# Up projections of two squared-relu MLPs: block products of seven quarter products instead of eight

## The chip, the cores and the metric

The kernel runs on one core of a Trainium2 chip, in one launch. Times are microseconds on the device. The core's engines run side by side and are ordered by semaphores: TensorE (PE: matmuls; PEld is its loading of the stationary operand), VectorE (DVE), ScalarE (ACT), GpSimd (POOL), and SyncE (SP), whose queue issues the large weight loads. Matmuls accumulate in PSUM banks; everything else lies in SBUF tiles of 128 partitions.

## What is computed

A first block (latent attention, banded attention and a hierarchical mixture of experts) feeds a second one of two layers. The second block ends each layer with a squared-relu MLP, and these two MLPs are all that the change is about:

```python
def sq_relu_mlp(h, w_up, w_down):
    return jnp.square(jax.nn.relu(h @ w_up)) @ w_down

def second_block(...):
    for l in range(DEPTH_2):                        # 2 layers
        h = rmsnorm(x, g_attn[l])
        x = x + dsa_mixer(h, ...) if l == 0 else x + nsa_mixer(h, ...)
        x = x + sq_relu_mlp(rmsnorm(x, g_mlp[l]), w_up[l], w_down[l])
        if l == 0:
            kv_shared = shared_kv(x, ...)
    return rmsnorm(x, g_final)
```

x has 512 tokens and 1024 features in float32; w_up is 1024x4096, w_down 4096x1024.

## The kernel before

**Layout.** The activations lie transposed: `xT[:, k]` is chunk k (128 of the 1024 features) by 512 tokens. A projection makes 128 output features by 512 tokens at a time, a feature block, by adding eight chunk products in one PSUM bank.

**Split float32.** Every float32 product is three matmuls of a faster float32 form (`mm3`): high by high, high by low, low by high part. `split` makes the two parts of a tile: a cast on ScalarE (L60), then a subtract of the tile and the cast on VectorE (L66). This is done for each weight tile of 128x1024 after its DMA (`wraw`, four buffers; `wload`), for the normalized input, and for each hidden block.

**One MLP.** `mlp(l)` takes the 32 hidden blocks in four groups q. A group is eight up blocks, which give hidden blocks `hidh`/`hidl`, then eight down steps that consume them and add to the residual. An up block is 24 matmuls of 512 columns (`proj_gen`); its evacuation `ev_up` is relu on ScalarE, square on VectorE, and a split. `proj_gen` splits the weight of block n+1 while it issues block n. In the second MLP the down projection has the hidden blocks as stationary operand, and the residual is first transposed to token-major tiles `xn`.

**Around it.** The normalization has no pass of its own. `norm_block` scales the residual by the gain and splits it (`xh`, `xl`) as each block of the attention's output projection (`a_w_o`, `b_w_o`) arrives; the row statistics are applied after the down projection (`rb2`, `rn2`, squares of the reciprocal deviation, since squared relu is homogeneous). `hook1` computes these statistics during the first group, after up block 1; `hook2`, after up block 3, makes the broadcast (first MLP) or the 32 transposes and eight ScalarE copies (second).

**Order.** A tile scheduler keeps, on each engine, an order of its own for the instructions that this code issues, and adds the semaphores. Each engine runs its list in that order. X, O and P are pools of tiles of 128x512; a pool's next tile waits for the last reader of the one that it replaces.

Of the kernel before, what the change touches and what calls it, by code (L numbers as in the profile page):

```python
# [34 lines left out]
class Kern:  # L35
# [20 lines left out]
    def split(self, src, hi, lo, scale=None, pool=False):  # L56

        nc = self.nc
        if scale is None:
            nc.scalar.copy(hi, src)  # L60
        else:
            nc.scalar.activation(out=hi, in_=src, func=AF.Copy, scale=scale)
        if pool:
            return nc.gpsimd.tensor_tensor(out=lo, in0=src, in1=fv(hi), op=OP.subtract)  # L64
        if scale is None:
            return nc.vector.tensor_tensor(out=lo, in0=src, in1=fv(hi), op=OP.subtract)  # L66
        return nc.vector.scalar_tensor_tensor(out=lo, in0=src, scalar=scale, in1=fv(hi), op0=OP.mult, op1=OP.subtract)
# [116 lines left out]
            acc = self.square(acc, b, rows)  # L184
        return acc

    def norm(self, gain=None, both=None):

        st = Ctx()
        st.gain, st.both, st.acc, st.acc2, st.xh, st.xl = gain, both, None, None, [], []  # L190
        self.nx = st
        return st

    def norm_block(self, k):
        st, x = self.nx, self.xT[:, k]
        if st.gain is not None:
            st.xh.append(self.X("xh", F32R))
            st.xl.append(self.X("xl", F32R))
            self.split(x, st.xh[k], st.xl[k], st.gain[:, k:k + 1])
        st.acc = self.square(st.acc, x)  # L200
        if st.both is not None:
            st.acc2 = self.square(st.acc2, x, scale=st.both[:, k:k + 1], pool=True)

    def norm_nat(self, exp=False):
        st = self.nx
# [1013 lines left out]
    def dsa(self):  # L1219
        nc, A, xT, small = self.nc, self.A, self.xT, self.small  # L1220
        st = self.nx
# [23 lines left out]
        r1, r2, rr, rr2 = s4("r1"), s4("r2"), s4("rr"), s4("rr2")  # L1245
# [205 lines left out]
    def mlp(self, l):  # L1451
        nc, xT = self.nc, self.xT
        st = self.nx
        xh, xl = st.xh, st.xl
        if l == 0:
            self.norm(self.vec("g_kv_shared"))
        else:
            xn = [[None] * 2 for _ in range(4)]

        def hook1():  # L1460
            st.nat = self.nat_rstd(self.sums([st.acc]), D)
            if l == 1:
                st.rn2 = self.small.tile([128, 4], F32, tag="rn2", name="rn2")
                self.mul(st.rn2, st.nat, st.nat)

        def hook2():
            if l == 0:
                rb = self.bcast_rows(st.nat)
                st.rb2 = self.P("rb2", 1)
                self.mul(st.rb2, rb, rb)  # L1470
                return
            for t in range(4):
                for half in range(2):
                    pt = self.bank("t")
                    for k in range(4):
                        nc.tensor.transpose(pt[:, 128 * k:128 * k + 128], xT[:, 4 * half + k, 128 * t:128 * t + 128], self.ident)  # L1476
                    a = self.O("xn")
                    nc.scalar.copy(a, pt)
                    xn[t][half] = a
        if l == 1:  # L1480
            gf = self.ph.tile([128, D], F32, name="gf")
            g = self.A["g_final_2"]
            nc.sync.dma_start(gf, bass.AP(tensor=g.tensor, offset=g.offset, ap=[[0, 128], [1, D]]))
            ss = self.small.tile([128, 8], F32, tag="ssf", name="ssf")

        def finish(t0, t1):
            n = t1 - t0
            s4 = self.small.tile([128, n], F32, tag="s4", name="s4")
            v = ss[:, 2 * t0:2 * t1].rearrange("p (t h) -> p t h", h=2)
            nc.vector.tensor_tensor(out=s4, in0=v[:, :, 0], in1=v[:, :, 1], op=OP.add)  # L1490
            y = self.small.tile([128, n], F32, tag="y4", name="y4")
            self.col_rstd(s4, y, D)
            for t in range(t0, t1):

                a, b = xn[t]
                nc.scalar.activation(out=a, in_=a, func=AF.Copy, scale=y[:, t - t0:t - t0 + 1])
                nc.sync.dma_start(self.out[128 * t:128 * t + 128, 0:512], a)
                nc.vector.scalar_tensor_tensor(out=b, in0=b, scalar=y[:, t - t0:t - t0 + 1], in1=gf[:, 512:1024], op0=OP.mult, op1=OP.mult)
                nc.sync.dma_start(self.out[128 * t:128 * t + 128, 512:1024], b)

        for q in range(4):
            hh, hl = [], []

            def ev_up(b, ps):
                r = self.P("r", 2)
                nc.scalar.activation(out=r, in_=ps, func=AF.Relu)
                self.mul(r, r, r)
                a, c = self.X("hidh", F32R), self.X("hidl", F32R)
                self.split(r, a, c)
                hh.append(a)  # L1510
                hl.append(c)
            up = self.proj_gen(f"w_up{l}", range(8 * q, 8 * q + 8), xh, xl, ev_up)
            for n, _ in enumerate(up):
                if q == 0 and n == 1:
                    hook1()
                if q == 0 and n == 3:
                    hook2()
            if l == 0:
                def ev_down(b, ps):
                    b = b % 8  # L1520
                    t = self.P("dt", 2)
                    self.mul(t, ps, st.rb2)
                    nc.vector.tensor_tensor(out=xT[:, b], in0=xT[:, b], in1=t, op=OP.add)
                    if q == 3:
                        self.norm_block(b)
                self.proj_tr("w_down0", range(8 * q, 8 * q + 8), hh, hl, ev_down)
            else:
                for half in range(2):
                    last = q == 3 and half == 1
                    ps = [self.bank(g) for g in "sstt"]  # L1530
# [102 lines left out]
    def nsa(self, rb, kc, vc, kh, kl, vs):  # L1633
        nc, A, xT, ph = self.nc, self.A, self.xT, self.ph
# [158 lines left out]
def prep(inp):  # L1793
    g = {k: np.asarray(v) for k, v in inp.items()}
    m = {}
# [11 lines left out]
    o = np.arange(4000)  # L1807
# [24 lines left out]
    for l in range(2):  # L1832
        m[f"g_attn{l}"] = cols(g["g_attn_2"][l])
        m[f"g_mlp{l}"] = cols(g["g_mlp_2"][l])
        m[f"w_up{l}"] = chunks(g["w_up_2"][l])

    m["w_down0"] = g["w_down_2"][0].reshape(4, 8, 128, 8, 128).transpose(0, 3, 2, 1, 4).reshape(32, 128, 8, 128)

# [41 lines left out]
```

## Time and profile before

| | us |
|---|---|
| median of 3 runs | 2015.24 (2012.69 to 2016.48) |
| the profiled execution | 2013.01 |
| its span | 2011.2 |
| TensorE busy in it | 1915.0 (95%) |
| VectorE, ScalarE, GpSimd busy | 948.4, 733.1, 258.5 |
| mean granted TensorE clock | 0.977 of full speed |

The span runs from the first to the last recorded instruction; 1.8 us of the execution's time lie around it. The first MLP's up phases start at 1015.13, 1104.01, 1191.05 and 1278.09 us, with a down phase after each; those of the second at 1648.32, 1740.46, 1827.50 and 1914.54. Matmul records are longer than the distance between two matmuls, since matmuls overlap in TensorE: the pitch from start to start is what one costs.

### The profile page before, as it was taken

To read this page: it belongs to the slowest core of one execution; us is meant where nothing else is said; L and a number is where in the kernel's file an instruction comes from. 1 tells how busy PE (TensorE), PEld (TensorE's weight loads), DVE (VectorE), ACT (ScalarE), POOL (GpSimd) and SP (SyncE) were. 2 spreads that over 40 slices of the span, in tenths; PEclk is the share of its full clock that TensorE was granted. 3 is DMA by queue.
4 is the path that set the end of the run, shared out by engine and by line. 5 is a ranking of instruction groups with operands and counts; after the bars stand their busy time and mean duration, and the time that the engine had idled before them with its cause. 6 is when DMAs were issued, how large, how long until landed. Compare 5 with 4: busy or idle time off the path is not lost.

```text
span 2011.2 us, 26048 instructions
## 1 busy us (share of the span) xinstructions
PE 1915.0 (95%) x9802; PEld 1461.1 (73%) x9802; DVE 948.4 (47%) x2004; ACT 733.1 (36%) x1333; POOL 258.5 (13%) x330
## 2 busy tenths in 40 slices
PE   8999999979998867899999999999999999999998
PEld 6777778865544324558888888887789988888886
DVE  5677764461000025378454444465266554444343
ACT  3555552222111124357442323242355534233233
POOL 2212210020000024245100000000134300000001
PEclk9999999989999989799999999999999999999999
DMA  7523633138999994001233233224510032333221
GB/s 257 189 97 124 217 132 117 62 136 347 356 369 384 369 383 163 32 16 39 84 94 95 95 102 98 95 95 146 177 46 32 22 105 84 94 97 103 95 94 64
DMA packets 88224, 286.76 MB, mean 143 GB/s; under 512 B 12128, under 2 KB 13152, under 8 KB 88096
## 3 DMA queue, kind: packets, MB, share of 16 engines
q1 hardware_dynamic: 82624, 273.01, 39.1%
q10 hardware_dynamic: 4320, 7.87, 1.0%
q0 software_dynamic: 1152, 4.19, 0.6%
q8 instruction: 79, 1.29, 0.3%
q14 instruction: 49, 0.40, 0.1%
HBM read 274.02 MB, written 11.01 MB: 142 GB/s over the span
## 4 chain that ended last, share of the span: by engine, by line
PE 57%; DVE 2%; POOL 1%; issue 0%; ACT 0%; DVEq 0%; POOLq 0%; ACTq 0%
PE mm L49 37%; PE s L49 8%; PE o L49 5%; PE t L49 5%; PE t L244 1%; DVE sc L1336 0%; DVE p L230 0%; DVE m L1335 0%; POOL dw L1318 0%; PE t L1476 0%; DVE dg L162 0%; POOL cql L64 0%; POOL wl L64 0%; DVE wl L66 0%; DVE selb L1340 0%
## 5 line engine op out<-in xcount | busy, mean ns | idle before, releaser
L60 ACT CAST wh<-wr 128x1024 fp32r<-128x1024 f32 (+1 forms) x222 | 230.9, 1041 | 579.3 <-PE mm L49 303.7
L66 DVE TENSOR_TENSOR wl<-wr,wh 128x1024 fp32r<-128x1024 f32 (+1 forms) x216 | 264.0, 1222 | 312.7 <-ACT wh L60 311.8
L49 PE MATMUL mm<-xh,wh 128*128 128x512 f32 (+1 forms) x640 | 252.7, 395 | 0.0
L49 PE MATMUL mm<-xh,wl 128*128 128x512 f32 (+1 forms) x640 | 250.4, 391 | 0.0
L49 PE MATMUL mm<-xl,wh 128*128 128x512 f32 (+1 forms) x640 | 250.0, 391 | 0.0
L49 PE MATMUL s<-wm,xg 128*64 128x512 f32 x544 | 142.2, 609 | 11.6 <-DMA wm<-in_w_gu 11.6
L49 PEld LDWEIGHTS mm<-xh,wh 128*128 128x128 f32 (+1 forms) x640 | 120.0, 188 | 28.2 <-issue 2.2
L49 PEld LDWEIGHTS mm<-xh,wl 128*128 128x128 f32 (+1 forms) x640 | 120.0, 188 | 26.0
L49 PEld LDWEIGHTS mm<-xl,wh 128*128 128x128 f32 (+1 forms) x640 | 120.0, 187 | 25.3 <-issue 0.5
L233 ACT ACTIVATE p<-p,mx 128x128 f32<-128x128 f32 (+3 forms) x160 | 89.7, 561 | 93.5 <-DVE mx L232 89.4
L49 PEld LDWEIGHTS s<-wm,xg 128*64 128x64 f32 x544 | 43.3, 140 | 90.8 <-issue 66.4
L970 DVE TENSOR_TENSOR hid<-hid,s 128x256 f32<-128x256 f32 x17 | 7.2, 421 | 205.9 <-ACT hid L969 205.9
L49 PE MATMUL mm<-hidh,wh 128*128 128x512 f32 x256 | 99.6, 389 | 0.0
L49 PE MATMUL mm<-hidl,wh 128*128 128x512 f32 x256 | 99.6, 389 | 0.0
L49 PE MATMUL mm<-hidh,wl 128*128 128x512 f32 x256 | 99.6, 389 | 0.0
L235 POOL TENSOR_SCALAR p<-p,mx 128x128 f32<-128x128 f32 (+3 forms) x96 | 59.4, 622 | 156.5 <-DVE mx L234 111.7
L49 PE MATMUL mm<-hh,wh 128*128 128x512 f32 x192 | 77.9, 407 | 1.1 <-ACT hh L60 1.1
L49 PE MATMUL mm<-hl,wh 128*128 128x512 f32 x192 | 76.0, 396 | 0.8 <-DVE hl L66 0.8
L49 PE MATMUL mm<-hh,wl 128*128 128x512 f32 x192 | 75.4, 393 | 0.0
L49 PE MATMUL mm<-d,h2h 128*128 128x256 f32 (+1 forms) x288 | 70.5, 289 | 3.8 <-ACT xg L1011 2.8
L230 DVE CUSTOM_DVE_ANT_0 p<-s,ms 128x256 f32<-128x256 f32 (+3 forms) x128 | 61.2, 487 | 24.1 <-PE s L49 22.1
L244 PE MATMUL t<-ident,p 128*128 128x128 f32 x400 | 68.5, 278 | 3.8 <-POOL p L235 3.7
(575 smaller groups left out, 3995.8 us busy)
## 6 DMA issues: line engine op xcount, KB each, us to landing
wm<-in_w_gu SPq DMA_DIRECT2D x136, 512.0 KB, 7.1
wm<-in_w_dn SPq DMA_DIRECT2D x68, 512.0 KB, 7.4
wr<-in_w_up SPq DMA_DIRECT2D x64, 512.0 KB, 3.5
wr<-in_w_down SPq DMA_DIRECT2D x64, 512.0 KB, 3.5
wr<-in_w_ada SPq DMA_DIRECT2D x48, 512.0 KB, 4.1
wr<-in_w_in SPq DMA_DIRECT2D x22, 512.0 KB, 3.6
wr<-in_cmp_w SPq DMA_DIRECT2D x16, 512.0 KB, 3.8
ydr<-y ACTq DMA_DIRECT2D x30, 256.0 KB, 6.3
```

The source lines that it names most:

```text
L49: self.nc.tensor.matmul(ps, lhsT=l, rhs=r, start=start, stop=stop)
L60: nc.scalar.copy(hi, src)
L66: return nc.vector.tensor_tensor(out=lo, in0=src, in1=fv(hi), op=OP.subtract)
L230: nc.vector.tensor_tensor_reduce(out=p[:, :n], in0=s[:, :n], in1=master[:, c0:c0 + n], scale=1.0, scalar=-3.0e38, op0=OP.add, op1=OP.max, ...
L233: nc.scalar.activation(out=p[:, :n], in_=p[:, :n], func=AF.Exp, bias=mx[:, 1:2], accum_out=mx[:, 2:3])
L235: nc.gpsimd.tensor_scalar(p[:, :n], p[:, :n], mx[:, 3:4], 1.0 if gate is None else gate, op0=OP.mult, op1=OP.mult)
L244: nc.tensor.transpose(ps[:, b], p[:, b], self.ident)
L970: nc.vector.tensor_tensor(out=hid, in0=hid, in1=ps[:, 256:512], op=OP.mult)
```

## The change

The up projection takes the feature blocks in pairs. Features (K) are divided into even and odd chunks, the pair into its two blocks, the tokens into two halves of 256: a 2x2 block product, which is made of seven quarter products instead of eight, each of 4 chunks and 256 columns. For this, sums of weight quarters (`weights7`, on GpSimd) and differences of input quarters (`factors`, on GpSimd, made where `norm_block` made `xh` and `xl`) are split as before, and the seven products are combined into the two blocks by ScalarE copies, VectorE adds with an operand in PSUM and GpSimd adds (`products7`). The order of the products is 1, 2, 6, 5, 3, 7, 4. The weights are laid out with the even chunks first (`echunks`).

```diff
     def norm_block(self, k):
         st, x = self.nx, self.xT[:, k]
-        if st.gain is not None:
+        if st.x7 is not None:
+            self.factors(st.x7, k, x, st.gain[:, k:k + 1])
+        elif st.gain is not None:
...
+    def factors(self, x7, k, x, scale):
...
+        f = self.O("f")
+        nc.scalar.activation(out=f, in_=x, func=AF.Copy, scale=scale)
+
+        def pair(space, n1, n2, j1, j2, src):
+            hi, lo = space("xh", F32R), space("xl", F32R)
+            self.split(src, hi, lo)
+            x7.f[n1][j1], x7.f[n2][j2] = (hi[:, a], lo[:, a]), (hi[:, b], lo[:, b])
+        sub = lambda out, p, q: nc.gpsimd.tensor_tensor(out=out, in0=p, in1=q, op=OP.subtract)
+        if k % 2 == 0:
...
+            self.split(f[:, a], *[t[:, c] for t in x7.t0])
+            x7.f[1][j] = x7.t0[0][:, c], x7.t0[1][:, c]
+            x7.even, x7.t12 = f, self.O("t12")
+            sub(x7.t12[:, a], f[:, b], f[:, a])
+            return
+        pair(self.X, 2, 3, j, j, f)
+        t12, t43 = x7.t12, self.O("t43")
+        sub(t12[:, b], f[:, b], t12[:, a])
+        pair(self.X, 5, 6, j, j, t12)
+        sub(t43[:, b], f[:, b], x7.even[:, b])
+        sub(t43[:, a], f[:, a], t12[:, b])
+        pair(self.X, 4, 7, j, j, t43)
+
+    def weights7(self, name, b0, b1):
+        nc = self.nc
+        r0, r1 = self.wraw(name, b0), self.wraw(name, b1)
+        tt = lambda out, p, q, op: nc.gpsimd.tensor_tensor(out=out, in0=p, in1=q, op=op)
+        e, o = slice(0, 4), slice(4, 8)
+        s12, s34 = [self.ph.tile([128, 8, 128], F32, tag="ws", name="ws", bufs=2) for _ in range(2)]
+        tt(s12[:, e], r1[:, e], r1[:, o], OP.add)
+        tt(s12[:, o], s12[:, e], r0[:, e], OP.subtract)
...
+        split(self.wp, "w", 2, r0, 1, 2)
+        yield
+        tt(s34[:, e], r0[:, e], r1[:, e], OP.subtract)
+        tt(s34[:, o], r0[:, o], s12[:, o], OP.subtract)
+        split(self.ph, "s", 3, s12, 5, 6)
+        yield
+        split(self.ph, "s", 3, r1[:, o], 4, None)
+        split(self.ph, "s", 3, s34, 7, 3)
+        yield w
...
+            def product(n):
...
+                ps = self.bank(("mm", "s", "t")[banks % 3], (128, 256))
+                banks += 1
+                for j in range(4):
+                    self.mm3(ps, w[n][0][:, j], w[n][1][:, j], *x7.f[n][j], j == 0, j == 3)
+                return ps
...
+            c1, c2 = self.C("c"), self.C("c")
+            p1 = part(product(1))
+            add(c1[:, a], product(2), p1)
+            next(ahead, None)
+            u2 = part(product(6))
+            add(u2, u2, p1, True)
+            p5 = part(product(5))
+            u4 = add(part(), u2, p5, True)
+            add(c1[:, b], product(3), u4)
+            evac(bs[0], c1)
+            next(ahead, None)
+            u3 = add(part(), product(7), u2)
+            add(c2[:, b], u3, p5, True)
+            add(c2[:, a], product(4), u3)
+            evac(bs[1], c2)
+            yield
...
         if l == 1:
...
+            hook2()
...
-            def ev_up(b, ps):
-                r = self.P("r", 2)
-                nc.scalar.activation(out=r, in_=ps, func=AF.Relu)
-                self.mul(r, r, r)
-                a, c = self.X("hidh", F32R), self.X("hidl", F32R)
-                self.split(r, a, c)
...
+            def ev_up(b, c):
+                if b % 2:
+                    nc.vector.scalar_tensor_tensor(out=c, in0=c, scalar=0.0, in1=c, op0=OP.max, op1=OP.mult)
+                else:
+                    nc.scalar.activation(out=c, in_=c, func=AF.Relu)
+                    nc.scalar.activation(out=c, in_=c, func=AF.Square)
...
+            up = self.products7(f"w_up{l}", [(b, b + 1) for b in range(8 * q, 8 * q + 8, 2)], st.x7, ev_up)
             for n, _ in enumerate(up):
-                if q == 0 and n == 1:
+                if q == 0 and n == 0:
                     hook1()
-                if q == 0 and n == 3:
+                if q == 0 and n == 1 and l == 0:
                     hook2()
```

`part(src)` is a ScalarE copy of a product to SBUF, and `add(..., True)` an add on GpSimd. Left out of the diff are the places where buffers now lie, and the final gain, whose load is issued after the last group's up blocks instead of at the MLP's start.

What this makes of VectorE's list at the end of a down phase and the start of the next up phase of MLP 1 (`dt` and `xT` are the down step's residual update, `wl` the low part of a weight tile). Before:

```order
L1175 TENSOR_TENSOR dt<-mm,rb_8906 128x512
L1523 TENSOR_TENSOR xT<-xT,dt 128x512
L66 TENSOR_TENSOR wl<-wr,wh 128x1024 x2
L1175 TENSOR_TENSOR r<-r 128x512
L66 TENSOR_TENSOR hidl<-r,hidh 128x512
L66 TENSOR_TENSOR wl<-wr,wh 128x1024
```

After, the stretch of one pair in the first group of that MLP (`sl` is the low part of a weight sum or of the odd half of the second block's weight, `u` and `c` are 256-column parts; `mm`, `s` and `t` are the banks that the products take in turn):

```order
L300 TENSOR_TENSOR c<-s,u 128x256
L300 TENSOR_TENSOR u<-t,u 128x256
L66 TENSOR_TENSOR sl<-wr,sh 128x512
L300 TENSOR_TENSOR c<-mm,u 128x256
L1621 SCALAR_TENSOR_TENSOR c<-c 128x512
L66 TENSOR_TENSOR sl<-ws,sh 128x1024
L66 TENSOR_TENSOR hidl<-c,hidh 128x512 x2
L300 TENSOR_TENSOR c<-t,u 128x256
L66 TENSOR_TENSOR wl<-wr,wh 128x1024
L66 TENSOR_TENSOR sl<-ws,sh 128x1024
```

Per pair VectorE had six instructions (two `wl`, two `r`, two `hidl`) and has eleven; the subtract of the sum `ws` that the fifth product reads stands behind the evacuation of the pair before.

GpSimd's list has no row between the attention and the end of the second MLP before; its last ones are the attention's `p` and the final gain:

```order
L235 TENSOR_SCALAR p<-p,mx,gate 128x128 x2
L235 TENSOR_SCALAR p<-p,mx,gate 128x256 x2
L235 TENSOR_SCALAR p<-p,mx,gate 128x384 x2
L235 TENSOR_SCALAR p<-p,mx,gate 128x512 x2
L1547 TENSOR_TENSOR xn<-xn,gf 128x512 x4
```

After, in the middle of a group (`ws` are the weight sums):

```order
L300 TENSOR_TENSOR u<-u 128x256 x2
L249 TENSOR_TENSOR ws<-wr 128x512
L249 TENSOR_TENSOR ws<-ws,wr 128x512
L300 TENSOR_TENSOR c<-u 128x256
L249 TENSOR_TENSOR ws<-wr 128x512
L249 TENSOR_TENSOR ws<-wr,ws 128x512
```

Each pair puts four weight sums and three adds there, and the sums of the next pair stand between the adds of this one.

## Rows read from the trace of the kernel before

**Rows 1.** The page, busy time by engine and the granted clock in 40 slices.

```profile
PE 1915.0 (95%) x9802; PEld 1461.1 (73%) x9802; DVE 948.4 (47%) x2004; ACT 733.1 (36%) x1333; POOL 258.5 (13%) x330
...
PEclk9999999989999989799999999999999999999999
```

**Rows 2.** Windows of up phases, first and plain; header line gives the columns.

```profile
core 0: us, PE busy (x) PEld busy (x) DVE busy (x) ACT busy (x) POOL busy (x), PEclk, DMA share, GB/s
1015.13:1060.49 45.36, 45.36 (x203) 37.31 (x202) 22.88 (x33) 19.24 (x27) 0.00 (x0) 1.00 0.31 93
1104.01:1147.53 43.52, 43.52 (x193) 36.04 (x192) 20.16 (x24) 16.20 (x22) 0.00 (x0) 1.00 0.31 99
...
1648.32:1696.94 48.62, 48.62 (x233) 40.10 (x232) 21.74 (x32) 22.83 (x34) 0.00 (x0) 1.00 0.28 87
```

**Rows 3.** Timeline: first matmuls of an up and its down phase; start, duration, engine, line.

```profile
1104.01 0.39 PE L49 MATMUL mm<-xh,wh 128*128 128x512 f32 x1
...
1147.53 0.39 PE L49 MATMUL mm<-hidh,wh 128*128 128x512 f32 x1
```

**Rows 4.** Timeline of TensorE in the shared-KV phase: matmuls of 256 columns, 93 steps.

```profile
1427.50 0.28 PE L49 MATMUL mm<-wh,xl 128*128 128x256 f32 x1
...
1438.65 0.28 PE L49 MATMUL mm<-wh,xl 128*128 128x256 f32 x1
```

**Rows 5.** Lines by form: the weight loads of that phase; busy us, mean ns.

```profile
L49 PEld LDWEIGHTS mm<-wh,xl 128*128 128x128 f32 x64 | 12.3, 192 | 0.0
```

**Rows 6.** Lines by form, ScalarE.

```profile
L60 ACT CAST wh<-wr 128x1024 fp32r<-128x1024 f32 x213 | 223.9, 1052 | 573.7 <-PE mm L49 303.7 <-PE t L49 117.6 <-issue 78.4
L60 ACT CAST hidh<-r 128x512 fp32r<-128x512 f32 x64 | 39.7, 621 | 85.0 <-DVE r L1175 85.0
...
L62 ACT ACTIVATE xh<-xT,v_g_mlp 128x512 fp32r<-128x512 f32 x16 | 11.5, 719 | 0.0
...
L979 ACT COPY ht<-o 128x256 f32<-128x256 f32 x17 | 6.4, 374 | 13.1 <-PE o L977 13.1
...
L1478 ACT COPY xn<-t 128x512 f32<-128x512 f32 x8 | 4.4, 590 | 0.9 <-PE t L1476 0.9
```

**Rows 7.** Lines by form, VectorE.

```profile
L66 DVE TENSOR_TENSOR wl<-wr,wh 128x1024 fp32r<-128x1024 f32 x207 | 256.0, 1237 | 309.5 <-ACT wh L60 308.7
L66 DVE TENSOR_TENSOR hidl<-r,hidh 128x512 fp32r<-128x512 f32 x64 | 44.3, 692 | 42.4 <-ACT hidh L60 42.3
...
L67 DVE SCALAR_TENSOR_TENSOR xl<-xT,v_g_mlp,xh 128x512 fp32r<-128x512 f32 x16 | 12.0, 747 | 0.0
...
L970 DVE TENSOR_TENSOR hid<-hid,s 128x256 f32<-128x256 f32 x17 | 7.2, 421 | 205.9 <-ACT hid L969 205.9
```

**Rows 8.** Lines by form, GpSimd.

```profile
L64 POOL TENSOR_TENSOR h2l<-h,h2h 128x512 fp32r<-128x512 f32 x8 | 10.2, 1284 | 22.6 <-ACT h2h L60 22.4
...
L64 POOL TENSOR_TENSOR wf<-wm,wf 128x288 fp32r<-128x288 f32 x2 | 1.6, 798 | 272.3 <-ACT wf L60 272.3
```

**Rows 9.** Timeline near the end of MLP 2: GpSimd and VectorE at once.

```profile
1980.95 1.30 POOL L1547 TENSOR_TENSOR xn<-xn,gf 128x512 f32<-128x512 f32 x1
...
1982.20 2.28 POOL L1547 TENSOR_TENSOR xn<-xn,gf 128x512 f32<-128x512 f32 x1
...
1980.03 0.75 DVE L1541 SCALAR_TENSOR_TENSOR xn<-t,rn,xn 128x512 f32<-128x512 f32 x1 [0.61 <-PE t L49]
1981.21 2.13 DVE L66 TENSOR_TENSOR wl<-wr,wh 128x1024 fp32r<-128x1024 f32 x1 [0.43 <-ACT wh L60]
```

**Rows 10.** Timeline of an up block in MLP 1: a cast, its subtract, the next.

```profile
1020.59 1.05 ACT L60 CAST wh<-wr 128x1024 fp32r<-128x1024 f32 x1 [3.23 <-issue]
...
1021.67 1.23 DVE L66 TENSOR_TENSOR wl<-wr,wh 128x1024 fp32r<-128x1024 f32 x1 [2.95 <-ACT wh L60]
1022.82 0.69 DVE L1175 TENSOR_TENSOR r<-r 128x512 f32<-128x512 f32 x1
```

**Rows 11.** Timeline of ScalarE there: the table load of the row statistics.

```profile
1027.59 1.28 ACT L130 ACT_TABLE_LOAD   x1
```

More of the change, by code (lines that the diff above doesn't have):

```diff
@@ L185, in sumsq, with norm @@
         return acc
-    def norm(self, gain=None, both=None):
+    def norm(self, gain=None, both=None, quarters=False):
         st = Ctx()
+        st.x7 = Ctx() if quarters else None
         st.gain, st.both, st.acc, st.acc2, st.xh, st.xl = gain, both, None, None, [], []
@@ L202, in norm_block @@
             st.acc2 = self.square(st.acc2, x, scale=st.both[:, k:k + 1], pool=True)
+    def factors(self, x7, k, x, scale):
+        nc, j = self.nc, k // 2
+        a, b = slice(0, 256), slice(256, 512)
+        if k == 0:
+            x7.f = {n: [None] * 4 for n in range(1, 8)}
+        f = self.O("f")
[6 more added lines that the diff above has]
+        if k % 2 == 0:
+            if j % 2 == 0:
+                x7.t0 = self.O("xh", F32R), self.O("xl", F32R)
+            c = (a, b)[j % 2]
+            self.split(f[:, a], *[t[:, c] for t in x7.t0])
[10 more added lines that the diff above has]
+        pair(self.X, 4, 7, j, j, t43)
@@ new lines, in weights7, with split @@
+    def weights7(self, name, b0, b1):
[6 more added lines that the diff above has]
+        tt(s12[:, o], s12[:, e], r0[:, e], OP.subtract)
+        w = {}
+        def split(pool, tag, bufs, src, n1, n2):
+            hi, lo = [pool.tile([128, 8, 128], F32R, tag=tag + x, name=tag + x, bufs=bufs) for x in "hl"]
+            n = src.shape[1]
+            self.split(src, hi[:, :n], lo[:, :n])
+            w[n1] = hi[:, e], lo[:, e]
+            if n2:
+                w[n2] = hi[:, o], lo[:, o]
+        split(self.wp, "w", 2, r0, 1, 2)
[7 more added lines that the diff above has]
+        yield w
@@ new lines, in products7, with part, add @@
+    def products7(self, name, pairs, x7, evac):
+        nc = self.nc
+        a, b = slice(0, 256), slice(256, 512)
+        pairs = list(pairs)
+        ahead = self.weights7(name, *pairs[0])
+        banks = 0
+        for m, bs in enumerate(pairs):
+            for w in ahead:
+                pass
+            ahead = self.weights7(name, *pairs[m + 1]) if m + 1 < len(pairs) else iter(())
+            def product(n):
+                nonlocal banks
+                ps = self.bank(("mm", "s", "t")[banks % 3], (128, 256))
[3 more added lines that the diff above has]
+                return ps
+            def part(src=None):
+                t = self.ph.tile([128, 256], F32, tag="u", name="u", bufs=6)
+                if src is not None:
+                    nc.scalar.copy(t, src)
+                return t
+            def add(out, p, q, pool=False):
+                (nc.gpsimd if pool else nc.vector).tensor_tensor(out=out, in0=p, in1=q, op=OP.add)
+                return out
+            c1, c2 = self.C("c"), self.C("c")
[14 more added lines that the diff above has]
+            yield
@@ L1468, in hook2 @@
                 rb = self.bcast_rows(st.nat)
[L1469 to L1470 removed]
+                self.mul(rb, rb, rb)
+                st.rb2 = rb
                 return
@@ L1476, in hook2 @@
                         nc.tensor.transpose(pt[:, 128 * k:128 * k + 128], xT[:, 4 * half + k, 128 * t:128 * t + 128], self.ident)
-                    a = self.O("xn")
+                    a = (self.O, self.X)[half]("xn")
                     nc.scalar.copy(a, pt)
@@ L1754, in chunks, with echunks @@
     return w.reshape(K // 128, 128, N // n, n).transpose(2, 1, 0, 3)
+def echunks(w):
+    return chunks(w)[:, :, [0, 2, 4, 6, 1, 3, 5, 7]]
 def kchunks(w, n, kk):
@@ L1834, in prep @@
         m[f"g_mlp{l}"] = cols(g["g_mlp_2"][l])
-        m[f"w_up{l}"] = chunks(g["w_up_2"][l])
+        m[f"w_up{l}"] = echunks(g["w_up_2"][l])
     m["w_down0"] = g["w_down_2"][0].reshape(4, 8, 128, 8, 128).transpose(0, 3, 2, 1, 4).reshape(32, 128, 8, 128)
```

32 lines of the change are left out of this document (18 added, 14 removed).

## The prediction

> **What bounds the kernel now.** I read the shares of the page first: TensorE is busy for 1915.0 us of the span, and the granted clock stands at 9 tenths or more in the slices that hold the two MLPs [rows 1], and at 1.00, the 2.4 GHz level, in the windows of their up phases [rows 2]. The windows of the up phases came next, since an average over the span says nothing of one stage. In each of them TensorE is busy from end to end: a plain phase of eight up blocks is 43.52 us with 43.52 us of TensorE work, while VectorE has 20.16, ScalarE 16.20 and GpSimd nothing [rows 2]. So TensorE is the bound there, and the reader is to see the idle GpSimd: the change gives it work. The phase holds 8 blocks x 24 = 192 matmuls, and from the first to the start of the next phase 43.52 us pass [rows 3]: 0.2267 us a matmul of 512 columns. The DMAs take 0.28 to 0.31 of the DMA engines there [rows 2] and stay out of the sum.
>
> **What is removed and added on TensorE.** Before, a pair of feature blocks is 48 matmuls of 512 columns, 48 x 0.2267 = 10.88 us. After, it is 7 products x 4 chunks x 3 = 84 matmuls of 256 columns. Another phase of this kernel runs 256-column matmuls with a new 128x128 weight each: 93 steps between the two rows shown take 11.15 us, 0.1199 us each [rows 4]. A pair is then 84 x 0.1199 = 10.07 us, 0.81 less; with 32 pairs (8 phases of 4) that is -25.8 us, and a phase without a wait is 40.3 us. So half the columns cost 0.53 of the time, and 7/8 becomes 0.926.
>
> The load row says the mean weight load is 192 ns [rows 5], more than the pitch, so in that phase loads lie beside matmuls and beside one another. The Trainium skill, "TensorE: Matmul & The Clock Gate", The mechanism, says a weight load overlaps a running matmul only where it goes to another row group, and these matmuls all use the whole array. Its price is the third rival; the pitch of [rows 4] speaks against the rule as it stands.
>
> **What is added on the other engines, per pair.** The durations are the forms nearest in shape. ScalarE: three weight casts of 1024 (1.052 each) and one of 512 (0.621), three copies PSUM to SBUF of 256 (0.374), relu and square of one block and two hidden casts (0.62 each) [rows 6]: 3.16 + 0.62 + 1.12 + 2.48 = 7.4 us. VectorE: three 1024 subtracts (1.237), three 512 subtracts (0.692, one of the odd weights, two of the hidden block), a two-input 512 operation (0.747), four 256 adds with one operand in PSUM (0.421) [rows 7]: 3.71 + 2.08 + 0.75 + 1.68 = 8.2 us. GpSimd: four weight sums of 128x512 at 1.284, three adds of 256 columns. The slope from 288 to 512 columns, (1284 - 798)/224 = 2.17 ns a column, gives 0.73 for 256 [rows 8]: 5.14 + 2.19 = 7.3 us. Each engine alone fits in 10.07. Taken alone they would all be hidden by TensorE.
>
> **But VectorE and GpSimd don't run side by side.** GpSimd works at 1980.95 and ends at 1982.25. A VectorE subtract of two SBUF inputs, normally 1.237, starts at 1981.21 and takes 2.13: it ends at 1983.34, 1.09 after GpSimd. GpSimd's next one starts at 1982.20 and takes 2.28, ending at 1984.48, 1.14 after the subtract. They take turns, 2.23 us for one of each [rows 9]. In the same stretch the VectorE operation with an operand in PSUM takes its normal 0.75 with GpSimd running. So the PSUM adds stay outside, and everything else of VectorE and all of GpSimd's work form one serial loop. In turns a 1024 subtract costs 1.09 and a weight sum 1.14, each 0.14 to 0.15 under its full length; taking the same off the shorter forms gives 0.55 for a 512 subtract, 0.60 for the two-input 512 operation and 0.59 for a 256 add (estimates). VectorE: 3 x 1.09 + 3 x 0.55 + 0.60 = 5.52. GpSimd: 4 x 1.14 + 3 x 0.59 = 6.33. Together 11.85 us a pair, more than TensorE's 10.07. With full durations it is 3.71 + 2.08 + 0.75 + 7.33 = 13.86. These are the two ends for the loop's period. I take 12.3, near the lower end because [rows 9] show the turns themselves: 11.85 and 0.45 for about six places in a pair where the next holder first waits for ScalarE or for a product. What such a handover costs is in [rows 10]: the cast ends at 1021.64 and the subtract starts at 1021.67, and the subtract's successor starts 0.08 before it ends.
>
> The Trainium skill, "SBUF — State Buffer", SBUF: two separate sides, states this rule: a VectorE operation with two SBUF inputs and a GpSimd operation that reads SBUF exclude one another for the whole instruction. The turns of [rows 9] agree; that the loser is blocked for the whole instruction would make the period 13.86, whereas the rows charge 2.23 for a pair that is 2.52 by full lengths.
>
> **What that loop delays.** The first pair of a phase is prepared while the down blocks before it run, so the loop's deficit falls on three pairs. The latest thing it makes is the low half of the fourth weight sum (s34), read by the third matmul of the fifth product, product 3. I walked one phase through the instruction order, with t = 0 at the first product. The loop has been free of gaps since t = 7; the subtract of s34 ends at 14.3 for the second pair, needed at 16.1: no wait. At 26.65 for the third, needed at 26.16: TensorE waits 0.5. At 37.95 for the fourth, needed at 36.24 + 0.5: 1.2. So 1.75 us a phase at a period of 12.3. The same walk gives about 2.5 us of wait for each us of period, and none below 11.6: wait = 2.5 x (period - 11.6). After the last product the hidden blocks 6 and 7 are wanted 18 matmuls into the down block and later (4 us), which covers a relu, square, cast and subtract (3 x 0.62 + 0.69). So 8 x 1.75 = +14.0 us, with ends of 8 x 0.6 = 5 (period 11.85) and 8 x 5.65 = 45 (13.86).
>
> **The first phase of each MLP.** Seven factors are now made from the normalized input ahead of it instead of one pair of tiles. In MLP 1 the chain of the last attention output block is an add (0.69), the scaled copy (0.72), GpSimd's subtracts (0.73 each), casts and subtracts (0.62, 0.69) [rows 6 to 8]. Before, it was needed at the 22nd matmul of 512, 4.8 us on; now the first product wants it at the tenth of 256, 1.1 us on. I put 1.6 us on that and 1.5 on the table load (1.283, [rows 11]) with the row statistics, which now stand in front of pair 2's casts: 3.1. In MLP 2 the transposes come ahead of the products and their eight copies (0.59, [rows 6]) queue behind the factors' casts on ScalarE: 1.9. Together +5.0, bounds 0 (all behind the last attention blocks) and 9. The statistics and transposes on TensorE themselves, 45.36 - 43.52 and 48.62 - 43.52 [rows 2], stay.
>
> Moved at no cost: the final gain's load is issued after the last up phase into freed tiles and hides behind the 22 us of the last phase's first down half (half of the phase's 43.52) before it is read; without that cover it would be one transfer, once. The factor subtracts on GpSimd stop nothing there but their own chain.
>
> **Sum.** -25.8 + 14.0 + 5.0 = -6.8 us. The profiled execution is 2013.01 us (span 2011.2 and 1.8 around it), which gives 2006.2; the median of the runs is 2.2 above it, so I forecast 2008.5.
>
> **Rivals.** (A) No wait: the loop stays near or under 11.85, or slack that I missed takes it up. For it: each engine has 2 us to spare. Against: [rows 9]. With 0 to 8 us of waits and 0 to 5 of prologue, -25.8 to -13: 1989.4 to 2002. (B) Slower: the loop's period is above 12.84, because changes of holder cost more than I charged or because a semaphore comes late while the other side holds on. Place: the s34 subtract, TensorE waiting before product 3. Price: 8 x 2.5 us for each us of period. The break-even is a wait of (25.8 - 5.0)/8 = 2.6 a phase, a period of 12.64; at 13.3 the sum is -25.8 + 34 + 5 = +13.2, 2028, and at 13.86 +24.4, 2039.6. For it: only one stretch of the profile shows such turns, three operations long. Against: those turns are shorter than full lengths. (C) The 256-column matmul is bound by its weight load here: 84 x 0.192 = 16.1 us a pair, +5.25 x 32 = +168, 2183. Against: [rows 4], the same shape at 0.1199.
>
> By the Trainium skill's rule on row groups, in the section named above, (C) would hold.
>
> **How the numbers follow.** Forecast (period 12.0 to 12.84, -12.8 to +4 us): 0.52, of it 0.18 within 4 us of no change. (A) 0.19. (B) 0.27. (C) 0.01. Another mishap without sign: 0.01. About 0.2%, 4 us, is what a measurement of this kernel can tell from no change. Faster is 0.34 + 0.19 = 0.53, the same 0.18 + 0.01 = 0.19, slower 0.27 + 0.01 = 0.28. The range 1996 to 2026 leaves out the lower half of (A) and the upper third of (B). The forecast's own range is 2002 to 2019.
>
> **What would show it.** Up phases of about 42 us in the windows after, against 40.3 (A) and over 43.5 (B). TensorE idle before product 3 of the third and fourth pair, released by VectorE's sl subtract. The means of the wl and sl subtracts well above 1.24 us and of the GpSimd weight sums above 1.28, while the adds with a PSUM operand stay near 0.42. The matmuls of 256 columns at a pitch of 0.12. If VectorE and GpSimd keep their normal lengths, or the waits stand at ScalarE's copies instead, the argument is wrong.

## The result, and the profile after

The changed kernel takes 2026.98 us (median of 7, 2024.15 to 2034.25) against 2014.48 for the one before (median of 7, 2010.41 to 2016.48): ratio 1.0071, 95% interval 1.0054 to 1.0088. It is slower; faster was forecast, and the time lies 1 us above the range. The profiled execution took 2026.98 (span 2025.2).

The page first: busy time by engine, and the granted clock in 40 slices.

```profile
PE 1905.5 (94%) x10954; PEld 1499.7 (74%) x10954; DVE 1136.9 (56%) x2180; ACT 821.9 (41%) x1525; POOL 607.5 (30%) x586
...
PEclk9999999989999988699999999999999989999999
```

Against [rows 1] TensorE is busy for less (1905.5 for 1915.0), so work did go, but the span grew by 14.0 us: TensorE waits. GpSimd more than doubled. Where it waits is read from windows cut at the phases' first matmuls. The forecast had put nothing on the attention's output projection before each MLP (the output phase), so here are the windows of these two phases in the kernel before (columns as in [rows 2]):

```profile
971.54:1015.13 43.59, 43.59 (x194) 36.10 (x194) 23.66 (x30) 16.91 (x23) 0.00 (x0) 1.00 0.30 97
1595.63:1648.32 52.69, 52.69 (x267) 44.40 (x266) 27.62 (x53) 20.86 (x35) 2.83 (x4) 1.00 0.24 80
```

And the changed kernel: output, first up, first down and second up phase of MLP 1, then output, first and second up phase of MLP 2.

```profile
968.81:1018.63 49.82, 45.92 (x195) 36.91 (x194) 37.98 (x37) 24.23 (x37) 26.39 (x20) 0.97 0.28 85
1018.63:1066.59 47.96, 44.43 (x347) 42.13 (x347) 42.27 (x54) 28.62 (x50) 28.19 (x23) 1.00 0.31 90
1066.59:1111.26 44.67, 44.19 (x194) 35.81 (x193) 27.00 (x29) 12.08 (x15) 14.20 (x9) 1.00 0.33 96
1111.26:1153.83 42.57, 40.91 (x337) 40.46 (x336) 33.92 (x40) 22.81 (x39) 26.16 (x19) 1.00 0.32 99
1602.23:1661.51 59.28, 55.59 (x273) 45.70 (x273) 39.42 (x60) 28.19 (x49) 29.30 (x24) 0.97 0.22 63
1661.51:1714.33 52.82, 47.94 (x370) 46.91 (x371) 40.71 (x53) 32.90 (x57) 29.36 (x24) 0.94 0.28 83
...
1757.88:1800.13 42.25, 40.58 (x337) 40.37 (x336) 34.59 (x39) 23.00 (x39) 25.13 (x20) 1.00 0.32 98
```

The balance against before, phase by phase: the six plain up phases -0.95 three times, -1.27, -1.00 and -1.26, together -6.4. The two output phases +6.2 and +6.6, the two first up phases +2.6 and +4.2, together +19.6. The four down phases of MLP 1 +1.15, +1.06, +1.03 and +0.15, together +3.4. That is +16.6; work ahead of the MLPs ended 2.7 earlier in this execution, which leaves the 14.0 of the spans. (In MLP 2, 0.7 of the output phase's 6.6 is seven transposes that now stand ahead of the first product and were in the first up phase before.)

In a plain up phase the waits are the forecast ones. The forms on VectorE and GpSimd (count, busy us and mean ns):

```profile
L66 DVE TENSOR_TENSOR wl<-wr,wh 128x1024 fp32r<-128x1024 f32 x175 | 247.0, 1411 | 129.7 <-ACT wh L60 128.9
L66 DVE TENSOR_TENSOR sl<-ws,sh 128x1024 fp32r<-128x1024 f32 x64 | 89.3, 1395 | 37.6 <-ACT sh L60 37.6
...
L300 DVE TENSOR_TENSOR c<-s,u 128x256 f32<-128x256 f32 x40 | 16.8, 420 | 14.0 <-POOL u L300 7.8 <-PE t L49 3.2 <-PE s L49 3.1
...
L249 POOL TENSOR_TENSOR ws<-wr 128x512 f32<-128x512 f32 x64 | 102.7, 1615 | 203.7 <-DMA wr<-in_w_up 171.1 <-DVE sl L66 32.7
L300 POOL TENSOR_TENSOR u<-u 128x256 f32<-128x256 f32 x64 | 84.2, 1315 | 104.8 <-ACT u L296 103.0
```

The subtracts rose from 1237 ns [rows 7] to about 1400, the weight sums to 1615 against 1284 [rows 8], and the adds with a PSUM operand stayed at 420. The subtract of s34 in the second up phase of MLP 1, whose first product starts at 1111.26 (VectorE's timeline), and the two matmuls that wait for it (TensorE's):

```profile
1124.48 1.22 DVE L66 TENSOR_TENSOR sl<-ws,sh 128x1024 fp32r<-128x1024 f32 x1
...
1136.94 1.22 DVE L66 TENSOR_TENSOR sl<-ws,sh 128x1024 fp32r<-128x1024 f32 x1
...
1148.39 1.22 DVE L66 TENSOR_TENSOR sl<-ws,sh 128x1024 fp32r<-128x1024 f32 x1
```

```profile
1138.21 0.39 PE L49 MATMUL mm<-xh,sl 128*128 128x256 f32 x1 [0.64 <-DVE sl L66]
...
1149.66 0.39 PE L49 MATMUL s<-xh,sl 128*128 128x256 f32 x1 [1.02 <-DVE sl L66]
```

They end 14.4, 26.9 and 38.4 us (1148.39 + 1.22 - 1111.26 = 38.35) after that start; 14.3, 26.65 and 37.95 were forecast, and waits of 0.5 and 1.2. The measured waits are 0.64 and 1.02, 1.66 together; the phase lost 42.57 - 40.31 = 2.26 by them, since the matmuls around each wait also start further apart than 0.12.

The output phase had not been walked. Here is its costliest wait on TensorE, in the rows of ScalarE, GpSimd and TensorE (the GpSimd rows start with the first weight sum of the phase):

```profile
996.95 1.05 ACT L60 CAST sh<-ws 128x1024 fp32r<-128x1024 f32 x1 [3.60 <-POOL ws L249]
1000.33 0.62 ACT L60 CAST xh<-t 128x512 fp32r<-128x512 f32 x1 [2.33 <-POOL t L227]
...
1002.84 1.04 ACT L60 CAST wh<-wr 128x1024 fp32r<-128x1024 f32 x1
```

```profile
991.69 3.52 POOL L249 TENSOR_TENSOR ws<-wr 128x512 f32<-128x512 f32 x2 [3.02 <-DMA wr<-in_w_up]
995.18 1.73 POOL L249 TENSOR_TENSOR ws<-ws,wr 128x512 f32<-128x512 f32 x1
996.99 1.62 POOL L249 TENSOR_TENSOR ws<-wr,ws 128x512 f32<-128x512 f32 x1
998.58 1.72 POOL L227 TENSOR_TENSOR t<-f,t 128x256 f32<-128x256 f32 x1
```

```profile
1003.93 0.50 PE L49 MATMUL mm<-oh,wh 128*128 128x512 f32 x1 [2.23 <-ACT wh L60]
...
1005.24 0.79 PE L49 MATMUL mm<-oh,wl 128*128 128x512 f32 x1 [0.57 <-DVE wl L66]
```

The output projection's own weight cast (1002.84) stands on ScalarE behind casts that waited for GpSimd, which makes weight sums of the coming MLP in turns with VectorE. The first of these sums starts 22.9 us into the phase, when its weight has landed. After the two waits TensorE ran at the 1.2 GHz level for a while (window, granted clock 0.50):

```profile
1005.24:1008.39 3.15, 3.15 (x8) 2.47 (x8) 3.15 (x3) 1.03 (x2) 2.32 (x3) 0.50 0.69 228
```

In MLP 2 the first up phase begins with the transposes of the residual, and one of them waits for VectorE's update of the last residual block (`xT`):

```profile
1664.63 0.48 PE L1591 MATMUL t<-ident,xT 128*128 128x128 f32 x1 [2.75 <-DVE xT L1848]
```

### The profile page after: what moved, and what is told of

Its sections match the earlier page's. It is cut to its first block, busy times and chain, and to the rows that moved or that the text cites. A ratio compares the mean times of both kernels' runs of the same rounds, so it can differ in the third digit from the quotient of the medians.

```text
span 2025.2 us, 29219 instructions
## 1 busy us (share of the span) xinstructions
PE 1905.5 (94%) x10954; PEld 1499.7 (74%) x10954; DVE 1136.9 (56%) x2180; ACT 821.9 (41%) x1525; POOL 607.5 (30%) x586
## 4 chain that ended last, share of the span: by engine, by line
PE 39%; DVE 7%; POOL 7%; issue 3%; ACT 3%; DMA 1%; DVEq 0%; POOLq 0%; SPq 0%; ACTq 0%
PE mm L49 16%; PE s L49 10%; PE t L49 6%; PE o L49 5%; POOL ws L249 4%; DVE sl L66 1%; POOL u L300 1%; DMA wr<-in_w_up 1%; ACT sh L60 1%; PE t L359 1%; DVE hidl L66 1%; DVE c L1621 1%; POOL t L227 1%; DVE wl L66 1%; DVE c L300 1%
## 5 line engine op out<-in xcount | busy, mean ns | idle before, releaser
L60 ACT CAST wh<-wr 128x1024 fp32r<-128x1024 f32 (+1 forms) x190 | 197.0, 1037 | 365.8 <-PE mm L49 176.1
L66 DVE TENSOR_TENSOR wl<-wr,wh 128x1024 fp32r<-128x1024 f32 (+1 forms) x184 | 255.0, 1386 | 133.7 <-ACT wh L60 132.9
L249 POOL TENSOR_TENSOR ws<-wr 128x512 f32<-128x512 f32 x64 | 102.7, 1615 | 203.7 <-DMA wr<-in_w_up 171.1
L49 PE MATMUL s<-wm,xg 128*64 128x512 f32 x544 | 143.4, 614 | 14.4 <-DMA wm<-in_w_gu 14.4
L300 POOL TENSOR_TENSOR u<-u 128x256 f32<-128x256 f32 x64 | 84.2, 1315 | 104.8 <-ACT u L296 103.0
L66 DVE TENSOR_TENSOR sl<-ws,sh 128x1024 fp32r<-128x1024 f32 x64 | 89.3, 1395 | 37.6 <-ACT sh L60 37.6
L49 PE MATMUL mm<-hidh,wl 128*128 128x512 f32 x256 | 99.9, 390 | 1.0 <-DVE wl L66 1.0
L49 PE MATMUL mm<-hidh,wh 128*128 128x512 f32 x256 | 99.9, 390 | 0.2
L49 PE MATMUL mm<-xh,wh 128*128 128x512 f32 (+2 forms) x224 | 80.9, 361 | 7.8 <-DVE c L300 6.7
L60 ACT CAST sh<-ws 128x1024 fp32r<-128x1024 f32 x64 | 66.8, 1044 | 46.6 <-POOL ws L249 35.8
L49 PE MATMUL mm<-xh,wl 128*128 128x512 f32 (+2 forms) x224 | 78.4, 350 | 0.6 <-DVE wl L66 0.6
L49 PE MATMUL mm<-xl,wh 128*128 128x512 f32 (+2 forms) x224 | 78.6, 351 | 0.3 <-DVE xl L66 0.3
```

The lines of the kernel that those rows point to most:

```text
L49: self.nc.tensor.matmul(ps, lhsT=l, rhs=r, start=start, stop=stop)
L249: tt = lambda out, p, q, op: nc.gpsimd.tensor_tensor(out=out, in0=p, in1=q, op=op)
L300: (nc.gpsimd if pool else nc.vector).tensor_tensor(out=out, in0=p, in1=q, op=OP.add)
```

## The experiments

Theory T1: GpSimd and VectorE take turns, and the whole of their shared work, the factors and the first pairs' weight sums included, is what TensorE waits for, in the output phases as in the up phases. Rivals: the factors' chain before the first product (T2), the order on the queues (T3), VectorE's own load (T4), GpSimd's own time (T5). The kernel before ran beside them at 2011.01 (e1 to e4) and 2012.32 (e5 to e7).

**e1, no weight sums.**

```diff
-        s12, s34 = [self.ph.tile([128, 8, 128], F32, tag="ws", name="ws", bufs=2) for _ in range(2)]
-        tt(s12[:, e], r1[:, e], r1[:, o], OP.add)
-        tt(s12[:, o], s12[:, e], r0[:, e], OP.subtract)
+        s12, s34 = r1, r0
...
-        tt(s34[:, e], r0[:, e], r1[:, e], OP.subtract)
-        tt(s34[:, o], r0[:, o], s12[:, o], OP.subtract)
```

> The four weight sums of a pair on GpSimd are left out; raw weight quarters are split in their place, so the casts, subtracts and matmuls stay and the values of the up projection change. Theory T1 (GpSimd and VectorE take turns; all the loop's work, the factors' included, is what TensorE waits for): a pair loses 4 x 1.14 = 4.6 us of loop, 12.3 - 4.6 = 7.7, under 10.07: plain up phases fall from 42.3-42.6 to 40.5-40.8, down phases of MLP 1 from 44.6 to 43.6, and the attention output phases (49.8 and 59.3; 43.6 and 52.7 before the change) lose their 8 sums (9 us of loop) and come to within 2 us of the kernel before; about 2003 to 2008 in all. Rival T2 (it is the factors' own chain, made block by block before the first product, not the amount of shared work): the output phases and first up phases stay 15 us or more over the kernel before; about 2015 to 2018.

Measured: 1991.61 in one run. Output and first up phase of MLP 1, a plain up phase, output and first up phase of MLP 2:

```profile
971.73:1015.66 43.93, 43.90 (x194) 36.03 (x194) 34.40 (x39) 25.79 (x40) 14.37 (x13) 1.00 0.35 101
1015.66:1059.37 43.71, 42.74 (x347) 41.71 (x346) 33.35 (x52) 29.30 (x49) 16.72 (x15) 1.00 0.34 105
1102.92:1143.23 40.31, 40.31 (x337) 40.30 (x336) 27.68 (x41) 24.77 (x41) 13.63 (x12) 1.00 0.36 108
1585.14:1638.86 53.72, 53.68 (x274) 44.95 (x273) 38.87 (x63) 30.52 (x52) 17.11 (x17) 1.00 0.26 77
1638.86:1685.03 46.17, 44.79 (x373) 44.06 (x372) 32.78 (x51) 32.07 (x56) 14.04 (x15) 1.00 0.31 95
```

The plain phase is 40.31, what 336 matmuls at 0.12 take. The output phases are 0.3 and 1.0 over before and the first up phases 1.7 and 2.5 under, although every factor is still made on GpSimd: T2 falls. It beat even T1's range by 11 us: T1's figure had not counted the first up phases, which fell by 4.3 and 6.7 against the changed kernel (47.96 to 43.71, 52.82 to 46.17).

**e2, no factor differences.** The four GpSimd subtracts in `factors` go.

```diff
...
-            sub(x7.t12[:, a], f[:, b], f[:, a])
...
-        sub(t12[:, b], f[:, b], t12[:, a])
-        pair(self.X, 5, 6, j, j, t12)
-        sub(t43[:, b], f[:, b], x7.even[:, b])
-        sub(t43[:, a], f[:, a], t12[:, b])
-        pair(self.X, 4, 7, j, j, t43)
+        pair(self.X, 5, 6, j, j, f)
+        pair(self.X, 4, 7, j, j, x7.even)
```

> The factors' four subtracts of 128x256 per two blocks on GpSimd are left out and plain scaled input is split in their place, so casts, low-part subtracts and matmuls stay and the values of the up projection change. T1: an output phase loses 16 x 0.59 = 9.4 us of loop, as much as the eight weight sums that lie there; output plus first up phase, now +8.8 (MLP 1) and +10.8 (MLP 2) over before, fall to about half, 2017 in all. T2: both chains lose their GpSimd steps and output plus first up phase come to within 4 us of before, 2010. Plain up phases stay at 42.3 to 42.6 by both.

Measured: 2012.84 in one run. Output and first up phase of MLP 1, a plain up phase, and the same pair of MLP 2:

```profile
967.58:1012.30 44.72, 44.05 (x194) 35.85 (x194) 33.45 (x37) 23.89 (x37) 14.11 (x8) 1.00 0.32 95
1012.30:1058.80 46.50, 43.86 (x348) 41.98 (x347) 40.63 (x54) 28.63 (x50) 24.28 (x19) 1.00 0.33 93
1103.53:1146.11 42.58, 40.92 (x337) 40.48 (x336) 33.91 (x40) 22.83 (x39) 26.16 (x19) 1.00 0.33 99
1594.93:1649.44 54.51, 53.75 (x274) 44.96 (x273) 38.11 (x60) 28.45 (x50) 17.14 (x12) 1.00 0.23 68
1649.44:1700.23 50.79, 46.71 (x372) 45.68 (x371) 39.02 (x53) 32.06 (x57) 25.39 (x20) 0.97 0.29 85
```

The +19.6 fell to 1.13 + 1.14 + 1.82 + 2.17 = +6.3. That is 2.3 for MLP 1 and 4.0 for MLP 2, within T2's 4 us and not T1's half. Either removal takes away most of it, so it is the two loads together that TensorE waits for; by itself this run speaks for T2, and it is e1 that rules T2 out as the whole cause.

**e3, weight sums late.** All work is kept; the weight sums of the first two pairs of each MLP wait for the sixth and the last output block.

```diff
+        if b0 in (0, 2):
+            z = self.xT[:, 5 + b0, 0:1]
+            for s in (s12, s34):
+                tt(s[:, 0, 0:1], z, z, OP.add)
```

> The weight sums of the first two pairs of each MLP wait for the sixth and the last block of the attention output (a one-column add ahead of them); all work is kept. T1: the amount of shared work is the same and is paid later: output phases 45 to 47 and 54 to 56, first up phases 2 to 4 us longer, total within 3 us of the changed kernel (2024 to 2030). A rival T3 (the order on the queues: the output block's own weight cast stands on ScalarE behind a factor cast that waits for GpSimd behind the sums): the 2.2 and 2.5 us waits for the weight cast and the lower clock behind them go and don't come back: 4 to 8 us faster than the changed kernel, 2019 to 2023.

Measured: 2032.59, ratio to the kernel before 1.0118 (1.0093 to 1.0142). Output and first up phase of MLP 1:

```profile
969.06:1015.36 46.30, 43.75 (x195) 35.91 (x194) 31.16 (x35) 24.27 (x37) 19.50 (x18) 1.00 0.27 80
1015.36:1068.99 53.63, 48.97 (x346) 46.81 (x347) 47.41 (x56) 28.85 (x50) 35.92 (x29) 0.87 0.31 91
```

46.3 + 53.6 = 99.9 against 49.8 + 48.0 = 97.8 in the changed kernel. The output phase gains 3.5 and the next pays back 5.7, partly at a lower clock (0.87). This order only moves the wait, and in MLP 2 likewise (55.42 + 58.47 against 59.28 + 52.82): T3's gain of 4 to 8 us did not come. The total lies 3 us above T1's range, and the next phase pays more than the 2 to 4 us expected. Another order, with the output projection's own cast ahead of the others on ScalarE, was not tried.

**e4, weight sums on VectorE.**

```diff
-        tt = lambda out, p, q, op: nc.gpsimd.tensor_tensor(out=out, in0=p, in1=q, op=op)
+        tt = lambda out, p, q, op: nc.vector.tensor_tensor(out=out, in0=p, in1=q, op=op)
```

> The weight sums on VectorE instead of GpSimd, nothing else. T1: where the two take turns only the sum of both counts, and a 512-column sum is shorter on VectorE (0.61 from start to start against 1.14 in turn): the loop falls by 4 x 0.53 = 2.1 us a pair, under 11.6: plain up phases 40.5 to 41.2, output phases 46 to 47 and 55 to 56, 2010 to 2016 in all, no slower than the kernel before by more than 2 us. Rival T4 (no turns worth the name, each engine by itself): VectorE has 8.2 + 4 x 0.69 = 10.9 us a pair and becomes the bound; plain up phases 43.5 to 45, total 2028 to 2040.

Measured: 2002.41, ratio 0.9959 (0.9944 to 0.9975): 0.4% faster than before, and 8 us under T1's range. Output and first up phase of MLP 1, and a plain up phase of each MLP:

```profile
969.06:1013.81 44.75, 43.94 (x195) 36.02 (x194) 35.53 (x42) 24.82 (x37) 13.06 (x12) 1.00 0.32 95
1013.81:1062.26 48.45, 44.76 (x347) 43.26 (x346) 43.39 (x65) 29.60 (x51) 17.69 (x16) 0.96 0.33 95
1105.81:1146.54 40.73, 40.56 (x337) 40.35 (x336) 35.19 (x48) 22.79 (x39) 11.34 (x11) 1.00 0.32 96
...
1737.61:1777.93 40.32, 40.32 (x338) 40.31 (x337) 34.60 (x47) 24.60 (x40) 12.13 (x12) 1.00 0.33 99
```

More work on the busier engine made the kernel 1.2% faster than the changed one (2002.41 against 2026.98, of two series). T4 falls. The output phases come down to 1.2 and 1.8 over before, but the first up phases stay at 48.45 and 50.67, 3.1 and 2.05 over: moving the sums does not cure these.

**e5, memsets in place of the sums.**

```diff
-        tt = lambda out, p, q, op: nc.gpsimd.tensor_tensor(out=out, in0=p, in1=q, op=op)
+        def tt(out, p, q, op):
+            nc.gpsimd.memset(out, 1.0)
+            nc.gpsimd.memset(out, 0.5)
```

> Each weight sum on GpSimd is replaced by two memsets of the same tile, which read nothing (0.52 us each in the kernel before, 1.05 for the two against 1.28 for a sum), so GpSimd stays about as busy and the values of the up projection change. T1 in the form that turns are taken for reading SBUF: VectorE's subtracts fall back to 1.24 us, plain up phases to 40.3 to 40.6, total 1991 to 1998, as without the sums. Rival T5 (what costs is GpSimd's own time and queue, in front of its adds and behind the buffers): GpSimd still has 4 x 1.05 + 2.2 = 6.4 us a pair at the same places; most of the waits stay, 2015 to 2027.

Measured: 1998.97 in one run, of which some 6 us lie before the first output phase (it starts at 977.57; 971.54 before). Output phase of MLP 1 and a plain up phase:

```profile
977.57:1023.50 45.93, 45.93 (x193) 37.78 (x194) 33.35 (x37) 24.85 (x39) 16.41 (x17) 0.95 0.34 102
1110.77:1151.08 40.31, 40.31 (x338) 40.31 (x336) 29.56 (x41) 24.65 (x41) 25.26 (x38) 1.00 0.36 108
```

TensorE waits in neither. The output phase is 2.3 us longer than before at a lower clock, but that clock came with it: TensorE had stood at 0.53 since 972.00, 5.6 us ahead of the phase. The output phase of MLP 2 took 53.42 without a wait. GpSimd's forms, and VectorE's subtract:

```profile
L302 POOL TENSOR_TENSOR u<-u 128x256 f32<-128x256 f32 x64 | 74.9, 1170 | 169.3 <-ACT u L298 168.8
L251 POOL MEMSET ws<- 128x512 f32 x128 | 64.7, 525 | 0.1
L250 POOL MEMSET ws<- 128x512 f32 x128 | 63.4, 525 | 213.2 <-DVE sl L66 206.6 <-PE o L49 6.5
```

```profile
L66 DVE TENSOR_TENSOR wl<-wr,wh 128x1024 fp32r<-128x1024 f32 x175 | 217.7, 1244 | 151.6 <-ACT wh L60 150.6
```

The memsets keep their 525 ns beside VectorE, and the `wl` subtract is back at 1244, while the adds, which read, still take 1170 (0.73 us alone by the slope of [rows 8], an estimate). T5 falls: turns are taken where GpSimd reads. The memsets also no longer wait for the weights to land, as the sums did (the 3.02 above); e4, in which the sums still wait for them and the plain up phases lost nearly all their waits all the same, speaks against that as the cause there. The Trainium skill, "SBUF — State Buffer", SBUF: two separate sides, says so of VectorE operations with two SBUF inputs (only against a GpSimd operation that reads SBUF); these rows agree with it.

**e7, factor differences on VectorE too** (e4, and in `factors`):

```diff
-        sub = lambda out, p, q: nc.gpsimd.tensor_tensor(out=out, in0=p, in1=q, op=OP.subtract)
+        sub = lambda out, p, q: nc.vector.tensor_tensor(out=out, in0=p, in1=q, op=OP.subtract)
```

> Weight sums and the factors' differences on VectorE, the adds of products left on GpSimd. Compared with the weight sums alone on VectorE (2002.4; output phases +1.2 and +1.8 over before, first up phases +3.1 and +2.0): T1: a difference costs 0.35 instead of 0.59 in turn and its two changes of engine go: output phases within 1 us of before, first up phases 1 to 2 us shorter than there, 1997 to 2001 in all; plain up phases stay 40.3 to 40.7. Rival (VectorE's order: each difference now waits in line behind low-part subtracts): no gain or up to 4 us lost, 2002 to 2007.

Measured: 1995.68, ratio 0.9919 (0.9897 to 0.9941). The output phases are 43.59 and 53.37, the first up phases 44.60 and 47.36, which is 3.9 and 3.3 shorter than in e4. T1 holds, the gain larger than expected: in the first up phases it was the differences on GpSimd that still delayed the products in e4.

**e6, nothing on GpSimd** (e7, and the adds of products):

```diff
-            u2 = part(product(6))
-            add(u2, u2, p1, True)
-            p5 = part(product(5))
-            u4 = add(part(), u2, p5, True)
+            u2 = add(part(), product(6), p1)
+            ps5 = product(5)
+            p5 = part(ps5)
+            u4 = add(part(), ps5, u2)
...
-            add(c2[:, b], u3, p5, True)
+            add(c2[:, b], u3, p5)
```

> Weight sums, factor differences and all adds on VectorE, two of the adds with a product straight from PSUM (their ScalarE copy goes); GpSimd has nothing in the MLPs. T1: no turns are left, and VectorE alone has, from start to start, 3 x 1.15 + 3 x 0.61 + 0.66 + 4 x 0.61 + 7 x 0.35 = 10.8 us a pair, over TensorE's 10.07 but under the 11.6 from which a phase waits: plain up phases 40.3 to 41, total 2000 to 2008, no better than with the adds left on GpSimd (2002.4). Rival: full lengths count and VectorE bounds (3.7 + 2.1 + 0.75 + 2.8 + 2.9 = 12.3 a pair): plain up phases 41.8 or more, 2015 or more.

Measured: 1990.55, ratio 0.9880 (0.9852 to 0.9908), the fastest version. Output, first up and a plain up phase of MLP 1, output and first up phase of MLP 2:

```profile
973.52:1017.13 43.61, 43.61 (x194) 36.10 (x194) 33.92 (x56) 25.90 (x40) 0.00 (x0) 1.00 0.33 98
1017.13:1060.19 43.06, 42.53 (x348) 41.73 (x347) 41.50 (x78) 27.39 (x43) 0.00 (x0) 1.00 0.29 86
1103.73:1144.05 40.32, 40.32 (x338) 40.31 (x337) 36.04 (x61) 24.21 (x37) 0.00 (x0) 1.00 0.37 108
1587.10:1640.49 53.39, 53.39 (x273) 45.04 (x273) 39.21 (x80) 30.36 (x52) 2.85 (x4) 1.00 0.26 78
1640.49:1685.50 45.01, 45.01 (x373) 44.11 (x371) 40.50 (x77) 30.53 (x50) 0.00 (x0) 1.00 0.28 80
```

The expectation of "no better than with the adds left on GpSimd" was wrong, by 9 us at the lower end of its range: it went by the plain phases, which could gain nothing more, and missed the first up phases, 48.45 and 50.67 in e4, 44.60 and 47.36 in e7 and now 43.06 and 45.01. VectorE is 96% busy in the first one (41.50 of 43.06), and TensorE idles there for only 0.53.

The two output and two first up phases together, against the kernel before: +19.6 in the changed kernel, -2.7 in e1, +6.3 in e2, +23.6 in e3, +8.1 in e4, -1.3 in e7, -5.2 in e6.

## Why the prediction was wrong

- **TensorE's own saving** was right: 40.31 us a plain up phase without waits (e1, e6) for the forecast 40.3, at a pitch of 0.12. The rival in which weight loads bound it, (C), is out.
- **The turns of VectorE and GpSimd, and what they delay** were right: the same subtract, the same matmul and pairs. The loss was 2.26 a phase in MLP 1 and 1.94 to 2.21 in MLP 2, not 1.75; six such phases gave -6.4 where 6 x (40.3 + 1.75 - 43.52) = -8.8 was forecast.
- **"The first phase of each MLP"** is the step that failed: "Together +5.0, bounds 0 (all behind the last attention blocks) and 9", with the loop's 1.75 a phase beside it. With it went two costs put at nothing: "The factor subtracts on GpSimd stop nothing there but their own chain", and the first pair's preparation, called done "while the down blocks before it run". Before the first phase there are no down blocks. Measured: +19.6 over the output and first up phases, where the two terms together, with 2 x -3.2 for TensorE's saving, made about +2. Of the 17.5 that is missing, 12.8 lies in the output phases, which had no term at all, 3.7 in the first up phase of MLP 2 and 1.0 in that of MLP 1. The chain of single operations behind the last output block was sized about right in MLP 1 (waits on the factors' casts and subtracts of 1.65 us in all, for the forecast 1.6). What it lacked is the turns ahead of it: the eight sums of two pairs and twelve of the sixteen factor differences stand in the output phase, with that phase's own two-input subtracts.
- **What the price list would have said:** by the forecast's own turn prices that loop has, per two blocks, two weight subtracts (2.18), three and a half 512 subtracts of factors (1.93), two square sums priced like a 512 subtract (1.10) and four differences (2.36), 7.6, times 4 is 30. With the eight sums (9.1) and the first pair's subtracts (3.82) it is 43, an estimate; 5.4 of it, the last two blocks' factors, comes only behind the phase. As an average that fits into 43.6. But no sum starts before 991.69, and what the trace then has in the last 26.9 us of the phase is, by the same prices, some 24.5 us of turns (an estimate), with ScalarE's casts between them. The loop is nearly full there, and the output projection's cast that stands behind it comes late.
- **What is shown of this, and what is open:** with the sums gone (e1), on VectorE (e4, e7) or not reading (e5), the waits of the output phases go, wholly or nearly; made later (e3), they move. Where the sums are on VectorE, the first up phases need the differences off GpSimd as well (e4 against e7). How much of the wait is the order on ScalarE, and how much the length of the turns, was not separated.
- **Cost put at nothing:** the first three down phases of MLP 1 got 1.0 to 1.2 each, most of it at one place, around a wait of 0.34 us for a `wl` subtract. Preparing the next phase's first pairs was counted as hidden there; without the sums on GpSimd the first one takes 43.55 (e1, e4, e5; 43.54 in e6).
- **A cost not in the sum:** the clock. The seven matmuls that start in the window at 0.50 took 3.15 us for the 1.59 of the normal pitch. The windows of MLP 2 with granted clocks of 0.97 and 0.94 hold such stretches too, each behind a wait of 2.5 to 2.8 us. How much of the +19.6 this is in all was not separated.
- **The slower rival (B)** had the sign but not the place: it needed a period above 12.84, and s34's subtracts came 12.46 and 11.45 us apart. Its break-even of a wait of 2.6 a phase was not reached in the plain phases; they were faster than before. That the time lies only 1 us outside the range is luck: the plain phases are near the forecast, and the place of the excess was in no rival.

## What to carry to other kernels

Before work is put on an idle GpSimd, add up in every stage, the ones that prepare the changed one above all, what it reads from SBUF and what VectorE reads from SBUF in two-input operations: here they took turns, and an engine that looks free was then no second engine. A sum of 1.28 us alone on GpSimd was cheaper on VectorE (0.71 to 0.82 in e4, 0.69 in e6) even though VectorE was the busier one. Where the shared work fills a stage, making a part of it later moved the wait (e3); less work in turns (e1), or all of it on one engine (e6), removed it.

## What was not expected of the hardware

GpSimd memsets of 128x512 kept 525 ns beside VectorE's two-input operations, where adds of half that size (128x256) took 1170 ns. And waits of 2.2 and 0.6 us on TensorE were followed by seven matmuls at half the granted clock, while the waits of 0.64 and 1.02 in the plain up phase left its clock at 1.00.
